# Hybrid encoder layer on one core: the first request's adaLN and projections by channel quarters

## The chip, the cores and the metric

The kernel runs on one core of a Trainium2 chip. The core has five engines that run their own instruction streams: TensorE (PE) for matmuls, VectorE (DVE), ScalarE (ACT), GpSimd (POOL), and SyncE (SP), which issues the DMAs here. The metric is the device time of one launch in microseconds (us), as the median of several runs. Lower is better.

## The reference

Two requests (1024 tokens of 1024 channels each, fp32) go through the same layer. What matters:

```python
mod = silu(c) @ w_ada + b_ada
shift, scale, gate = split(mod, 3)                       # 1024 channels each
h = rms_norm(x, norm_g) * (1 + scale) + shift
qa, ka, va, za, qb, kb, vb, zb, ga, gb = split(h @ w_in) # 512 128 128 512 512 512 512 512 1024 1024
oa = gqa_attention(rope(rms_norm(qa)), rope(rms_norm(ka)), va) * silu(za)   # branch A, 8 heads of 64
lam = exp(sum(lam_q1 * lam_k1)) - exp(sum(lam_q2 * lam_k2)) + lam_init
ob = rms_norm(diff_attention(rope(qb), rope(kb), vb, lam)) * silu(zb)       # branch B, 4 heads
merged = sigmoid(ga) * (oa @ w_proj_a) + sigmoid(gb) * (ob @ w_proj_b)
y = x + gate * (merged @ w_out)
```

`x` comes in transposed as well, so that `h` is made as 8 chunks of 128 channels (partitions) by tokens.

## The kernel before, in words

**Precision.** Most matmuls are made of three fp32r products: an operand is split into a high part (ACT copies it to fp32r) and a low part (DVE or POOL subtracts), and high x high, high x low, low x high are summed. So 8 channel chunks make 24 matmuls for one projection tile. AdaLN and the statistics are plain fp32.

**Stages.** The program does request 0 ("group 0"), then request 1. For a group: the head (`head`: keys and values `kva_gen`, the first half of the branch-A queries `qa_gen`, and some gate projections), attention in six phases (32 units of branch A, in two phases; 16 of branch B, in four), then merge and output. `kva_gen`, `qa_gen` and the branch-B projections work by token tiles (128 tokens by 256 columns, 24 matmuls each, in `proj_tt`, L514); behind the matmuls of a tile come the RMS statistics, rotary positions and transposes on ACT, DVE, POOL and PE. The gate projections (`z_gen`, L703) come in groups of 24 matmuls of 512 columns; 48 groups for a request, whose results go to memory (`zd`) until the merge.

**What sets the order.** `weave` draws matmul streams step by step, each at a share and with a lead from the tables at the top (`Z_SHARE`, `ATT_W`, `IN_A`, `Z_A` ...). It fills PE with projections while attention waits for its softmax. Three steps of `z_gen` are one group. A scheduler then sets the final order on each engine; each engine runs its own list strictly in order.

**The head of group 0.** `start` issues all loads on the SP queue. The shift and scale columns of `w_ada` are loaded as eight tiles of 512 rows by 512 columns (`load_ada`, L250): for channels 0 to 511 the shift, then the scale, then both for channels 512 to 1023. Loads of x (two halves of 512 tokens, `load_xT0`, L242) and the weights of keys and values stand among them. `ada` sums with the 2 columns of `silu(c)` as the stationary operand (L300: 32 matmuls with 2 output rows and 512 columns, each profiled as two instructions); `ada_end` copies the two rows, transposes them with four small matmuls (L309) and adds the bias. `inv_rms` sums the squares of a token half by one-column matmuls with `ones_c` (L273), `spread` broadcasts the result (L287, L289). `modulated` then makes `h` for four chunks at a time (L323 to L329), for the first token half only; `start_late` makes the second half after the first steps of the head. Thus nothing is projected before half of adaLN is done.

**Banks.** PSUM has two score banks of 1024 columns (`sbank`), three others (`fbank`) and one for values. `gbank` draws from both kinds while `alone` is set (outside attention).

## Time and profile before

| | |
|---|---|
| three runs | 1974.46, 1974.42, 1972.81 us; median 1974.42 |
| profiled execution | span 1971.9 us, 30870 instructions; the page gives no other time for it |
| PE | 1901.8 us busy (96%) |
| DVE | 1353.0 us (69%) |
| ACT | 1012.0 us (51%) |
| POOL | 680.9 us (35%) |
| DMA | 295.26 MB, mean 150 GB/s |
| mean granted PE clock | 0.990 |

"Busy" counts from an instruction's start to its modelled end, and matmuls are pipelined, so a PE that is busy all the time may still do little: the start-to-start time of dense matmuls tells their price. PEld is the load of the stationary operand. A row of the group views reads: line, engine, operation, output<-input by the program's names, shapes, count | busy us, mean ns of one | idle time of the engine before them and what ended it. A row of the waits reads: who waited <- for whom: us in total, times, longest.

### The profile page before, as it was taken

What the parts mean: (1) busy time and instruction counts of PE and PEld (TensorE: products, weight loads), DVE (VectorE), ACT (ScalarE), POOL (GpSimd) and SP (SyncE); (2) the same over time, 40 slices, a digit from 0 to 9 for tenths busy, and PEclk for the clock granted to TensorE, in tenths of its full rate; (3) what the DMA queues carried; (4) which work ended last, traced back from release to release, by engine and by line L of the source; (5) the groups of instructions that cost most, each with busy time, mean ns of one, the idle gap of its engine ahead of it and who ended that gap; (6) DMA issues with size and microseconds to landing.
All of it is one profiled execution on the core that took longest, in us unless ns stands there. A gap on an engine that the chain in (4) does not pass through costs nothing. (4 is left out here: it accounts for less than half of the span.)

```text
span 1971.9 us, 30870 instructions
## 1 busy us (share of the span) xinstructions
PE 1901.8 (96%) x10466; PEld 1619.1 (82%) x10466; DVE 1353.0 (69%) x2165; ACT 1012.0 (51%) x1920; POOL 680.9 (35%) x958
## 2 busy tenths in 40 slices
PE   8999999999989999999999999999999999998999
PEld 3888888888878985778889788888888889776887
DVE  4658876786888577757465598768878766776641
ACT  4447655565655353464323576556666444447410
POOL 2363511442446251322235344114444426322210
PEclk9899999999999999999999999999999999999999
DMA  9125545556454345865641355555555334478431
GB/s 315 33 89 149 144 139 149 158 156 174 127 144 111 89 117 173 272 234 179 222 151 44 115 144 167 148 149 157 156 152 161 98 102 119 120 222 267 166 102 75
DMA packets 271614, 295.26 MB, mean 150 GB/s; under 512 B 37856, under 2 KB 220256, under 8 KB 271456
## 3 DMA queue, kind: packets, MB, share of 16 engines
q1 hardware_dynamic: 271456, 293.28, 50.1%
q8 instruction: 84, 1.38, 0.3%
q14 instruction: 74, 0.61, 0.1%
HBM read 133.72 MB, written 42.01 MB: 89 GB/s over the span
## 5 line engine op out<-in xcount | busy, mean ns | idle before, releaser
L703 PE MATMUL f<-u,w 128*128 128x512 f32 x2184 | 561.3, 395 | 3.0 <-ACT w L179 1.3
L514 PE MATMUL f<-w,u 128*128 128x256 f32 x3456 | 489.6, 286 | 5.2 <-ACT ev L709 2.7
L514 PEld LDWEIGHTS f<-w,u 128*128 128x128 f32 x3456 | 460.7, 192 | 26.8 <-ACT ev L709 3.7
L703 PEld LDWEIGHTS f<-u,w 128*128 128x128 f32 x2184 | 396.8, 189 | 78.1 <-ACT w L179 1.8
L181 POOL TENSOR_TENSOR w<-st,w 128x512 fp32r<-128x512 f32 x166 | 227.8, 1391 | 463.2 <-ACT w L179 412.9
L736 DVE TENSOR_REDUCE m<-s 128x1 f32<-128x1024 f32 x256 | 310.2, 1217 | 55.1 <-PE s L735 52.0
L771 DVE STREAM_TRANSPOSE p<-p 128x1024 f32<-128x1024 f32 x192 | 238.0, 1241 | 112.8 <-ACT p L738 110.2
L785 DVE TENSOR_TENSOR q<-q,hi 128x512 fp32r<-128x512 f32 x256 | 193.9, 774 | 47.9 <-ACT hi L784 46.4
L738 ACT ACTIVATE p<-s,m,rsB 128x1024 f32<-128x1024 f32 x128 | 154.0, 1204 | 135.0 <-DVE m L737 103.3
L738 ACT ACTIVATE p<-s,m,rsA 128x1024 f32<-128x1024 f32 x128 | 153.8, 1202 | 128.1 <-DMA q<-p 95.8
L735 PE MATMUL s<-u,sw 128*128 128x512 f32 x512 | 205.0, 401 | 0.0
L784 ACT ACTIVATE hi<-q 128x512 fp32r<-128x512 f32 x256 | 153.2, 624 | 78.2 <-DMA q<-p 50.2
L179 ACT ACTIVATE w<-st 128x512 fp32r<-128x512 f32 x196 | 114.2, 626 | 101.9 <-DMA st<-in_w_in_dram 46.6
L976 PE MATMUL f<-u,w 128*128 128x512 f32 x552 | 136.4, 400 | 11.3 <-ACT ev L709 4.1
L796 PE MATMUL a<-hi,u 128*128 128x256 f32 x512 | 132.0, 284 | 4.8 <-DVE oo L813 3.1
L976 PEld LDWEIGHTS f<-u,w 128*128 128x128 f32 x552 | 104.8, 192 | 35.3 <-DVE u L987 4.6
L836 PE MATMUL a<-q,u 128*128 128x256 f32 x512 | 125.9, 385 | 5.6 <-DMA q<-p 1.9
L797 PE MATMUL a<-q,u 128*128 128x256 f32 x512 | 129.8, 287 | 0.5 <-DVE q L785 0.4
L734 PE MATMUL s<-u 128*128 128x512 f32 x256 | 109.5, 428 | 7.9 <-ACT p L738 4.0
L734 PE MATMUL s<-u,u 128*128 128x512 f32 x256 | 103.3, 404 | 13.8 <-ACT p L738 9.0
L836 PEld LDWEIGHTS a<-q,u 128*128 128x128 f32 x512 | 95.9, 193 | 21.6 <-issue 2.9
L735 PEld LDWEIGHTS s<-u,sw 128*128 128x128 f32 x512 | 97.4, 190 | 15.5
(186 smaller groups left out, 2639.1 us busy)
## 6 DMA issues: line engine op xcount, KB each, us to landing
q<-p SPq DMA_DIRECT2D x768, 128.0 KB, 2.6
st<-in_w_in_dram SPq DMA_DIRECT2D x132, 256.0 KB, 3.0
zd<-ev SPq DMA_DIRECT2D x96, 256.0 KB, 2.2
sw<-u SPq DMA_DIRECT2D x256, 64.0 KB, 2.0
p<-zd SPq DMA_DIRECT2D x64, 256.0 KB, 3.8
u<-in_w_ada_dram SPq DMA_DIRECT2D x8, 1024.0 KB, 10.4
st<-in_w_in_dram SPq DMA_DIRECT2D x64, 128.0 KB, 2.7
st<-in_w_out_dram SPq DMA_DIRECT2D x32, 256.0 KB, 3.2
```

Source lines behind the costliest of these rows:

```text
L181: e.tensor_tensor(out=wl, in0=st, in1=wh.bitcast(F32), op=ALU.subtract)
L514: nc.tensor.matmul(ps, lt[c][:, sl], w[:, c, wi, :], start=(k == 0), stop=(k == 23))
L703: nc.tensor.matmul(ps, w[:, c, wi, e * P : (e + 1) * P], rt[c], start=(k == 0), stop=(k == 23),)
L734: nc.tensor.matmul(s[:, sl], q, k[:, sl], start=True, stop=False)
L735: nc.tensor.matmul(s[:, sl], sw, k[:, sl], start=False, stop=True)
L736: nc.vector.tensor_reduce(out=m, in_=s, axis=AX.X, op=ALU.max, negate=True)
L738: nc.scalar.activation(pt.rearrange("p (j c a) -> p j c a", j=4, c=8), s.rearrange("p (c a j) -> p j c a", c=8, j=4), AF.Exp, scale=rs, bi ...
L771: nc.vector.transpose(pt, pt)
L784: nc.scalar.activation(th, tl.bitcast(F32), AF.Copy)
L785: nc.vector.tensor_tensor(out=tl, in0=tl.bitcast(F32), in1=th.bitcast(F32), op=ALU.subtract)
L836: nc.tensor.matmul(acc, u["v"][:, k], pT[:, k], start=(k == 0), stop=(k == 7))
L976: nc.tensor.matmul(ps, w[:, c, wi, d * P : (d + 1) * P], o[:, oi, :], start=(k == 0), stop=(k == 11))
```

## The change

AdaLN is done by quarters of 256 channels. `load_ada` loads, for a quarter, 512 rows by 256 columns of the shift and 256 of the scale into one tile. `ada` then gives each of four 128-row chunks its own 32-column strip of the PE array (`tile_position`), with `silu(c)` padded to 32 columns (`cpad`, in the `at` tile); the four partial sums land on four partition strips, are copied as one 128 x 512 tile, and are added and transposed by matmuls with `two`, a matrix of ones at rows j*32 and j*32+1. As soon as a quarter of shift and scale is there, `modulated` makes two chunks of `h` (the multiplication by 1/rms is inside it now, on DVE or POOL), and those two chunks are at once multiplied: `chunk_early` sums keys and values of all eight token tiles in the two score banks, `z_early` two gate groups (first 256 columns, first token half) in two of the other banks. Both token halves go this way (the second from quarter 1 on), so `start_late` is gone. `kva_gen` and the first `z_gen` take these sums as `given`; the weights of the second gate piece are loaded into two `u` tiles. While early sums are held, `gbank` draws only from `fbank`. The squares of the second half are added before the one-column products, as those of the first half were. The tables of shares and leads are set anew for both groups.

```diff
 Z_SHARE = (
-    (7, 19, 5, 3, 3, 4),
+    (6, 19, 5, 3, 2, 6),
     (9, 14, 7, 3, 2, 6),
 )
-    (1.15, 1.354, 1.035, 1.15, 0.85, 1.069),
+    (1.15, 1.188, 1.035, 1.15, 0.991, 1.069),
...
+Z_FIRST = (12, 6)
+Z_FIRST_A = (-0.15, 0.0)
...
-BEHIND = 1.4
-AHEAD = 100
+BEHIND = 1.45
+AHEAD = 99
...
-        if alone[0] and turn[0] % 5 in (0, 2):
+        if alone[0] and not early and turn[0] % 5 in (0, 2):
...
+    def ada(quarter, wts, cpad):
+
+        acc = gbank()
+        for q, wt in enumerate(wts):
+            for c in range(4):
+                nc.tensor.matmul(
+                    acc[32 * c : 32 * c + 32], cpad[:, q * 4 + c], wt[:, c], start=(q == 0), stop=(q == 1),
+                    tile_position=(0, 32 * c),
+                )
+        part = rtile()
+        nc.vector.tensor_copy(part, acc)
+        ps = gbank()[:, :8].rearrange("p (t c g) -> p t c g", t=2, g=2)
+        for third in range(2):
+            for c in range(2):
+                o = third * 256 + c * P
+                nc.tensor.matmul(ps[:, third, c], part[:, o : o + P], two, start=True, stop=True)
...
+    def chunk_early(ht, hf, c):
+
+        hh, hl = (x[c] for x in ht[hf][:2])
+        w = kva_w[0][0]
+        for tt in (1, 0, 3, 2) if c == NCH - 1 else range(4):
+            sl = slice(tt * P, (tt + 1) * P)
+            for k, (lt, wi) in enumerate(((hh, 0), (hh, 1), (hl, 0))):
+                first, last = c == 0 and k == 0, c == NCH - 1 and k == 2
+                mm = nc.tensor.matmul(
+                    early["kva"][hf * 4 + tt], lt[:, sl], w[c][:, wi, :],
+                    start=(first and tt % 2 == 0), stop=(last and tt % 2 == 0),
+                )
...
+        wts = [load_ada(n) for n in range(2)]
         kva_w.append(load_w(w_cols(w_in, (C_KA, 256)), early=True))
-        wts += [load_ada(n) for n in range(5, 8)]
+        wts += [load_ada(n) for n in range(2, 4)]
+        kva_w.append(load_w(w_cols(w_in, (C_ZA, 256)), early=True))
         xT.append(load_xT0(1))
...
+        wts += [load_ada(n) for n in range(4, 6)]
+
+        rsb = [spread(inv_rms(added(squares(xT[0]))))]
+        kva = [x[:, i : i + 256] for x in (sbank(), sbank()) for i in range(0, 1024, 256)]
+        early.update(kva=kva, z=[fbank(), fbank()])
+        for quarter in range(4):
+            ada(quarter, wts[quarter * 2 : quarter * 2 + 2], cpad)
+            if quarter < 2:
+                split_early(kva_w[quarter][1])
+            for hf in range(2):
+                if quarter == 0 and hf:
+                    continue
+                if quarter in ((0, 2), (1, 2))[hf]:
+                    add_h(ht, hf, quarter // 2)
+                    if hf and quarter == 1:
+                        rsb.append(spread(inv_rms(added(squares(xT[1])))))
+                cs = range(0 if hf and quarter == 1 else quarter * 2, quarter * 2 + 2)
+                modulated(ht, hf, xT[hf], cs, rsb[hf])
+                for c in cs:
+                    chunk_early(ht, hf, c)
+            for c in (range(0), range(4), range(4, 6), range(6, 8))[quarter]:
+                z_early(ht, c)
+            if quarter == 0:
+                wts += [load_ada(n) for n in range(6, 8)]
...
-            for i in range(2):
-                weave((islice(kva, 6), 6, 0.0), (islice(zs, 3), 3, 0.0))
-                if i == 0:
-                    late()
-            weave((chain(kva, qa), 40, 0.0), (islice(zs, nz - 6), nz - 6, Z_HEAD_A[g]))
+            drain(islice(zs, 6))
+            weave((kva, 27, 0.0), (islice(zs, Z_FIRST[0]), Z_FIRST[0], Z_FIRST_A[0]))
+            weave((qa, 27, 0.0), (islice(zs, Z_FIRST[1]), Z_FIRST[1], Z_FIRST_A[1]))
```

The order on the engines. First the SP queue at the end of the loads of the head, before: all adaLN tiles and x stand ahead of the tables (`gqa` to `p_1427`, the vectors of lambda).

```order
L250 DMA u_192<-in_w_ada_dram 128x4x512
L242 DMA u_194<-in_xT_prompt_dram 128x2x512 x2
L242 DMA u_195<-in_xT_prompt_dram 128x2x512 x2
L407 DMA gqa<-in_qn_a_dram 128x64
L407 DMA gka<-in_kn_a_dram 128x64
L441 DMA tab_396<-in_cosA_dram 128x8x64
L441 DMA tab_398<-in_sinA_dram 128x8x64
```

The same queue in the change, from the rotary tables of branch B on; `u_309` and `u_312` are the last adaLN quarter.

```order
L452 DMA cosB<-in_cosB_dram 128x8x16 x2
L452 DMA sinB<-in_sinB_dram 128x8x16 x2
L454 DMA gB<-in_qn_b_dram 128x64
L454 DMA gB<-in_kn_b_dram 128x64
L464 DMA p_1469<-in_lam_q_dram 128x64
L464 DMA p_1469<-in_lam_k_dram 128x64
L464 DMA p_1469<-in_lam_q_dram 128x64
L264 DMA u_309<-in_w_ada_dram 128x4x256 x2
L264 DMA u_312<-in_w_ada_dram 128x4x256 x2
L464 DMA p_1469<-in_lam_k_dram 128x64
L473 DMA subg<-in_subln_g_dram 128x1
```

The last adaLN quarter has moved behind all tables but the fourth lambda vector and `subg`.

DVE in the head, before: the last shift and scale (`modc`), the modulation of the last chunks (`u_170`) and their low parts (`u_332`) stand ahead of the branch-B tables and lambda.

```order
L313 TENSOR_TENSOR modc<-s_324,bcol 128x8
L317 TENSOR_TENSOR modc<-modc,gcol 128x8
L325 TENSOR_SCALAR u_170<-u_170,modc 128x512 x2
L329 TENSOR_TENSOR u_332<-u_170,u_331 128x512 x4
L181 TENSOR_TENSOR w_412<-st_417,w_412 128x2x256
L416 TENSOR_SCALAR gB<-gB 128x64
```

DVE in the change, from the copy of quarter 2's sums (`f_494`; quarters count from 0) to that of quarter 3's (`f_592`).

```order
L318 COPY row_503<-f_494 128x512
L466 TENSOR_TENSOR p_1469<-p_1469 128x128
L474 TENSOR_SCALAR subg<-subg 128x1
L469 TENSOR_REDUCE lam_116<-p_1469 128x2
L471 TENSOR_TENSOR nlam<-lam_116 128x1
L472 TENSOR_SCALAR nlam<-nlam 128x1
L326 TENSOR_TENSOR modc<-f_505,bcol 128x2x4
L329 TENSOR_TENSOR modc<-modc,gcol 128x4
L341 TENSOR_SCALAR u_171<-u_171,modc 128x512
L341 TENSOR_SCALAR u_203<-u_203,modc 128x512
L318 COPY row_601<-f_592 128x512
```

The lambda steps now stand between quarter 2's sums and the modulation of its chunks (`u_171` of the first token half, `u_203` of the second).

More of the change, by code (lines that the diff above doesn't have):

```diff
@@ L118 @@
     alone = [True]
+    early = {}
     turn = [0]
@@ L207, in load_w @@
                 split_w(w, q, st)
-        return (w, sts) if early else w
+        cols = [w[c // 2][:, c % 2] for c in range(NCH)]
+        return (cols, (w, sts)) if early else cols
     def w_cols(mat, *cols):
@@ L337, in add_h, with z_early @@
             part.extend(u[:, c] for c in range(4))
+    def chunk_early(ht, hf, c):
[8 more added lines that the diff above has]
+                    start=(first and tt % 2 == 0), stop=(last and tt % 2 == 0),
+                )
+                if first and tt % 2 or last and tt % 2 == 0:
+                    tc.keep_in_program_order(mm)
+    def z_early(ht, c):
+        hh, hl = (x[c] for x in ht[0][:2])
+        w = kva_w[1][0]
+        for e in range(2):
+            for k, (wi, rt) in enumerate(((0, hh), (0, hl), (1, hh))):
+                nc.tensor.matmul(
+                    early["z"][e], w[c][:, wi, e * P : (e + 1) * P], rt,
+                    start=(c == 0 and k == 0), stop=(c == NCH - 1 and k == 2),
+                )
     def start(ht):
+        cpad = mtile("at", [P, 256], bufs=1).rearrange("p (c m) -> p c m", c=NCH)
+        nc.vector.memset(cpad, 0.0)
         nc.scalar.activation(cT, ccol, AF.Silu)
-        wts = [load_ada(n) for n in range(2)]
+        nc.vector.tensor_copy(cpad[:, :, :2], cT)
         dma(bcol, t["b_col"])
@@ L502, in ht_gen, with proj_tt @@
             yield 1
-    def proj_tt(ht, w, tt):
+    def proj_tt(ht, w, tt, given={}):
+        if tt in given:
+            for _ in CUTS:
+                yield 1
+            if tt == NTT - 1:
+                early.pop("kva")
+            return given[tt]
         ps = fbank()[:, :256]
@@ L1090, in z_item @@
         if i < 2:
-            return z_gen(ht, C_ZA + i * 256, st["zd"], i * 2, fn)
+            col, w = C_ZA + i * 256, None
+            if early and i == 1:
+                w = load_w(w_cols(w_in, (col, 256)), room=(utile(), utile()))
+            return z_gen(ht, col, st["zd"], i * 2, fn, w)
         if i < 4:
@@ L1099 @@
     states = [new_state(0), new_state(1)]
[L1100 removed]
+    start(states[0]["ht"])
     load_tables()
```

146 lines of the change are left out of this document (59 added, 87 removed).

## The prediction

> **What bounds the kernel now.** I first read the busy time by stretches. The cuts are the first dense sums (42.4), the clock's recovery (60), the first scores (140.7), the fifth attention unit (176.3) and the last of the 32 branch-A units (514.8); columns are length, busy us of PE, PEld, DVE, ACT, POOL (instructions), granted clock, DMA share, GB/s.
>
> ```profile
> 0.00:42.40 42.40, 34.82 (x102) 9.23 (x102) 18.20 (x31) 17.18 (x29) 7.84 (x12) 1.00 1.01 357
> 42.40:60.00 17.60, 17.60 (x92) 16.72 (x91) 9.08 (x24) 7.28 (x12) 4.94 (x4) 0.62 0.34 81
> 60.00:140.70 80.70, 73.84 (x497) 67.89 (x495) 48.73 (x135) 40.11 (x105) 45.27 (x63) 0.98 0.16 50
> 140.70:176.30 35.60, 35.60 (x195) 31.05 (x196) 25.89 (x38) 24.54 (x39) 8.54 (x12) 0.95 0.51 139
> 176.30:514.80 338.50, 331.08 (x1939) 290.29 (x1938) 255.15 (x371) 203.00 (x392) 113.48 (x144) 1.00 0.55 153
> 514.80:593.80 79.00, 72.84 (x423) 63.76 (x422) 65.24 (x106) 44.57 (x90) 38.72 (x69) 0.96 0.49 131
> ```
>
> From 60 us on PE is busy nearly all the time and no other engine comes close: 331 of 338.5 us in the long stretch, where DVE has 255. Before 42.4 us the DMA engines are full. A busy PE there says little, so I next read what it runs, in the timeline of PE (start, length, line, count):
>
> ```profile
> 30.15 10.46 PE L300 MATMUL f<-u,cT 128*2 128x512 f32 x24
> 42.41 2.31 PE L514 MATMUL f<-w,u 128*128 128x256 f32 x12
> 47.23 8.09 PE L273 MATMUL f<-ones_c,q 128*128 128x1 f32 x50
> 55.18 4.19 PE L703 MATMUL s<-u,w 128*128 128x512 f32 x9
> 59.17 2.08 PE L514 MATMUL f<-w,u 128*128 128x256 f32 x12
> 97.34 5.18 PE L703 MATMUL f<-u,w 128*128 128x512 f32 x22
> 102.36 2.79 PE L514 MATMUL f<-w,u 128*128 128x256 f32 x22
> 111.57 3.14 PE L514 MATMUL f<-w,u 128*128 128x256 f32 x24
> 114.55 0.62 PE L703 MATMUL f<-u,w 128*128 128x512 f32 x2
> ```
>
> Up to 42.4 us PE runs only adaLN (L300) and statistics, no projection. Then 50 one-column sums (L273) take 8 us. From start to start, a dense gate matmul (L703) takes (102.36-97.34)/22 = 0.23 us and a dense projection matmul (L514) (114.55-111.57)/24 = 0.124 us. The same lines by stretch (first L514, then L703):
>
> ```profile
> 0.00:60.00 60.00, 5.73 (x27) 5.47 (x28) 0.89 0.81 276
> 60.00:140.70 80.70, 48.01 (x359) 46.28 (x357) 0.98 0.16 50
> 0.00:60.00 60.00, 4.19 (x9) 2.86 (x9) 0.89 0.81 276
> 60.00:140.70 80.70, 28.15 (x111) 19.88 (x111) 0.98 0.16 50
> ```
>
> So by 60 us PE has done 27 x 0.124 + 9 x 0.23 = 5.4 us of the work that has to be done anyway. From 60 to 140.7 it does 359 x 0.124 + 111 x 0.23 = 70.0 us of it in 80.7. The hole in this kernel is the first 60 us; behind it PE is the bound, so whatever matmuls are moved into the hole should come off the end.
>
> **What the change puts into the hole.** Keys and values (8 token tiles x 24 = 192 matmuls) and two gate groups (48) are summed as the quarters come: 192 x 0.124 + 48 x 0.23 = 34.8 us of PE work. AdaLN keeps its 64 profiled instructions, 16 a quarter. When is the last quarter done? That decides. First the transfers: the SP queue's timeline, one stretch of DMA, and the issues with their time to landing.
>
> ```profile
> 22.66 5.40 SPq L242 DMA_DIRECT2D u<-in_xT_prompt_dram x4
> 39.03 1.09 SPq L413 DMA_DIRECT2D cosB<-in_cosB_dram x2
> 45.53 0.35 SPq L425 DMA_DIRECT2D p<-in_lam_q_dram x1
> 46.87 0.43 SPq L425 DMA_DIRECT2D p<-in_lam_k_dram x1
> 30.00:35.00 5.00, 5.00 (x16) 1.15 (x16) 4.71 (x6) 1.70 (x3) 3.46 (x2) 1.00 1.05 409
> p<-in_lam_k_dram SPq DMA_DIRECT2D x2, 32.0 KB, 3.2
> ```
>
> At 409 GB/s 1 MB takes 2.56 us. Today all 14 MB stand ahead of the tables. DMAs take turns on eight semaphores, so an issue waits for the eighth before it, and the first cosB issue waits until 39.03 for the last piece of x. In the change only 12 MB stand ahead: 5.1 us less, and I add 1.1 us because the three small column loads now go ahead of the first big one. So cosB issues at about 35, and the first lambda vector 6.5 us later, as today, less 0.5 for the load of `subg` that moves behind: 41. Three lambda loads take 1.3, and then the last adaLN quarter is issued, at 42.3. Its 2 MB need 5.1 us and some 2 us to start (between nothing and the 3.2 us of a small load): landed at 49.4. The fourth lambda vector is issued behind it and lands right after, about 50. Nothing is gained by the shorter head of the queue: the last adaLN quarter arrives 10 us later than the last byte of today's 14 MB.
>
> **Who waits for that.** In DVE's new order the product of the lambda vectors, their reduction, and the subtraction that waits for ACT's exponential stand ahead of the shift and scale of quarter 2 (third of four), and those ahead of the copy of quarter 3's sums. Today's rows for this chain:
>
> ```profile
> 51.40 0.28 DVE L427 TENSOR_TENSOR p<-p 128x128 f32<-128x128 f32 x1
> 55.44 0.28 DVE L430 TENSOR_REDUCE lam<-p 128x2 f32<-128x128 f32 x1
> 55.75 0.20 ACT L431 ACTIVATE lam<-lam 128x2 f32<-128x2 f32 x1 [1.98 <-DVE lam L430]
> 56.41 0.15 DVE L433 TENSOR_SCALAR nlam<-nlam 128x1 f32<-128x1 f32 x1
> L329 DVE TENSOR_TENSOR u<-u,u 128x512 fp32r<-128x512 f32 x8 | 5.0, 680 | 1.1 <-ACT u L328 1.1
> L328 ACT ACTIVATE u<-u 128x512 fp32r<-128x512 f32 x8 | 4.5, 616 | 0.4 <-DVE u L325 0.4
> L325 DVE TENSOR_SCALAR u<-u,modc 128x512 f32<-128x512 f32 x4 | 2.0, 539 | 0.0
> L306 DVE COPY p<-f 2x512 f32<-2x512 f32 x3 | 2.0, 676 | 1.4 <-PE f L300 1.0 <-issue 0.4
> ```
>
> Reduction to end is 56.56-55.44 = 1.1 us, plus 0.3 for the product: lambda 50 to 51.4. Quarter 2 then takes 0.3 for its shift and scale (two L313/L317-sized steps), two modulations of 0.54, and 0.62 on ACT until its first matmuls can start, at about 53. (The first two quarters' 17.4 us of sums have some 30 us ahead of that.) DVE goes on with the copy of quarter 3 (0.68), four low parts (2.7), shift, scale and one weight split (1.1), two modulations (1.1), four low parts (2.7): 61. PE has two quarters left, each 48 x 0.124 + 12 x 0.23 = 8.7 us: 53 + 17.4 = 70, which DVE's 61 doesn't hold up. What is left of the head (6 gate groups, 144 x 0.23 = 33.1; 8 query tiles, 192 x 0.124 = 23.8; transposes about 2.5) is 59.4 us. Today's named waits of PE between 60 us and the first scores are these:
>
> ```profile
> PE f L514 <- ACT ev L709: 2.3, 1, 2.3
> PE s L734 <- DVE u L570: 2.1, 1, 2.1
> PE f L567 <- DVE row L556: 1.7, 2, 1.5
> PE f L567 <- POOL row L556: 0.7, 1, 0.7
> ```
>
> That is 6.8 us. I keep 5: the one before the first scores stays, and keys now come all at once to be normalised, with 6 gate groups on PE to cover them. First scores: 70 + 59.4 + 5 = 134.5, against 140.7: **6 us**. If that cover fails, POOL's share (45 us busy in this stretch now) comes into the path; 7 us more is the bound I allow. If no wait is left it is 5 us less.
>
> **What is done by then.** All 8 gate groups (192) stand ahead of the first scores, against 120 matmuls today: 72 x 0.23 = **16.6 us** that the attention phases no longer have to carry. They give it back only where PE is their bound. The first four units fall from 66 gate matmuls to 24 (and gain 6 projection ones): 8 us less for PE in a stretch of 35.6 in which DVE has 26 us, in a chain; I take half, so 4 are lost. The stretch at 514.8 to 593.8 gains 24 gate matmuls where PE has 6 us of idle time: 4 come back. New weights and leads move matmuls between other stretches with the same total. PE's idle time from 176.3 to 593.8 is 13.6 us, which bounds what they can win; I take 0, with 6 either way.
>
> **Other edits.** The square sums are added on DVE before one matmul for each tile, so 28 of the 32 one-column products of the second half go (part of L273's 8 us, inside the hole). The padded adaLN weights, the row `two`, the `mc` steps and the separate row tile cost under 2 us of DVE, beside transfers. The room for the second gate piece's weights in two `u` tiles moves its loads to rows that wait for nothing on PE. Nought for each; if the cover is gone, up to 2.
>
> AdaLN's column tiles have no row of before. Run one after another they cost 24 instructions in 10.46, so 0.43 x 16 = 6.9 us a quarter; side by side at best a quarter of that, 1.7. For the last quarter the second half counts, 3.4 or 0.9 us behind 49.4: 52.8 at worst against DVE's 51.4 for lambda, under 2 us on the path. I take 0. The Trainium skill (TensorE: Matmul & The Clock Gate, Part 3) measured 2.38 times for three column tiles of 32; by that, as an estimate, a quarter takes 2.9 us and the sum is unchanged. It also (TensorEngine Tiling (Array Packing), Key Properties) says that a change of tiling mode drains the array, which speaks against alternating such tiles with full matmuls; it gives no price, and no run here shows it yet.
>
> The clock: from 55.18 nine L703 took 59.17-55.18 = 4.0 us, 0.44 each, at the 0.62 mean of that stretch. Quarter 2's sums start after a wait, so some 3 us of them may run at half rate, 1.5 us. I count it in the 5 us of waits. The Trainium skill (TensorE: Matmul & The Clock Gate, Part 1) says an idle window of about 3.4 us halves the clock and a busy one restores it; by that it costs, as an estimate, 1.7 us for each restart, and only the last restart is on the path.
>
> **Sum.** 6 + 16.6 - 4 + 4 = 22.6 us off the span of 1971.9: 1949.3. The page has no time for the profiled execution beside its span; the median of the runs, 1974.42, is 2.5 above it. Forecast **1952**, own range 1944 to 1959.
>
> **The rivals.** *The tables don't hold the last quarter* (0.2): quarter 2 is modulated before lambda, and PE starts at about 45 on what has landed; the early sums then end at 62, 8 us earlier: 1944. For it: nothing in the data needs lambda. Against it: DVE runs in order, and the product is ahead.
>
> *The head stays as long* (0.13): with both score banks and two of three other banks held by early sums, one bank serves transposes, spreads and the next gate group; the waits of 6.8 us double, and the last quarter slips by the 7 us allowed. First scores at 143; only the 16.6 come, less 4: 1971.9 + 2 - 12.6 + 2.5 = 1964.
>
> *The attention phases are full twice over* (0.08), and this one is slower: where PE work falls, DVE's chain keeps the old time; where it rises, PE lengthens it. From the order, in stretches of four units, the stretches that gain matmuls sum to 10.5 us in the first group and 12.6 in the second (one has 25 gate matmuls more). 1971.9 - 6 + 23.1 + 2.5 = 1991. It decides from where the shortened stretches return under 17 of their losses. Against it: DVE's 255 of 338.5 us.
>
> *The change does nothing in the hole* (0.04): the early sums wait for one buffer until all of h is there; 1971 to 1975.
>
> **How the numbers follow.** The forecast holds 0.55. 0.2% is 3.9 us, about what a measurement tells from no change: faster means under 1970.5. Forecast, first and second rival are on that side: 0.88; same 0.04; slower 0.08. The range takes in the first two rivals with their half widths, 1938 to 1967.
>
> **What would show it.** Right: projection matmuls on PE from about 20 us, a DVE wait for the lambda load near 50, early sums ended near 70, first scores at 130 to 139, the 32 branch-A units of the first group 10 to 18 us shorter. Wrong: first scores after 141, or a second group that is more than 5 us longer.

## The result, and the profile after

The changed kernel takes 1972.49 us (median of 12 runs, 1970.91 to 1980.13); the kernel before took 1974.54 beside it. The ratio on record is 0.9998 (the two medians alone would give 0.9990), with a 95% interval of 0.9988 to 1.0009: no difference. The forecast was 1952, so the prediction was wrong. The profiled execution has a span of 1971.0 us, against 1971.9 before.

First the busy time by stretches of the changed kernel (columns as in the prediction: length, busy us of PE, PEld, DVE, ACT, POOL, granted clock, DMA share, GB/s). The cuts are where PE becomes dense (46.6), the first sums of quarter 2 (67), the first scores (145.6), the fifth unit, the 33rd, and group 0's tail from 746.5 up to group 1's first scores (1093.2); the stretch from the 33rd unit to the 36th stands ahead of that from the 33rd to the 44th, which holds it.

```profile
0.00:46.60 46.60, 22.08 (x116) 14.86 (x117) 27.30 (x35) 19.16 (x33) 18.55 (x20) 0.85 0.98 304
46.60:67.00 20.40, 19.51 (x117) 13.81 (x117) 14.32 (x29) 8.15 (x13) 6.89 (x4) 0.92 0.42 119
67.00:145.60 78.60, 76.40 (x482) 68.50 (x483) 47.96 (x125) 35.14 (x94) 41.32 (x59) 1.00 0.23 71
145.60:182.30 36.70, 29.15 (x166) 25.18 (x165) 29.58 (x44) 22.77 (x45) 16.75 (x21) 0.92 0.47 118
182.30:509.40 327.10, 322.62 (x1900) 283.73 (x1899) 258.51 (x372) 197.82 (x382) 106.75 (x138) 1.00 0.60 155
509.40:589.20 79.80, 74.91 (x438) 65.88 (x437) 63.22 (x103) 44.43 (x89) 37.98 (x66) 0.98 0.51 131
509.40:746.50 237.10, 230.52 (x1392) 204.10 (x1390) 176.66 (x296) 121.94 (x249) 110.77 (x205) 0.99 0.44 114
746.50:1093.20 346.70, 333.74 (x1653) 273.48 (x1653) 213.41 (x366) 149.10 (x270) 106.58 (x119) 0.99 0.57 182
1093.20:1971.00 877.80, 844.87 (x4610) 728.95 (x4608) 607.10 (x907) 451.26 (x829) 286.38 (x404) 0.99 0.53 146
```

The last two stretches of the kernel before, for comparison:

```profile
747.80:1096.00 348.20, 338.02 (x1671) 274.67 (x1670) 216.76 (x372) 148.38 (x274) 107.05 (x119) 1.00 0.55 182
1096.00:1971.90 875.90, 843.99 (x4610) 726.21 (x4608) 606.28 (x907) 451.68 (x829) 282.43 (x404) 0.99 0.50 146
```

The first scores come at 145.6, 4.9 us later than before, not 6 earlier. From there to the end it is 1825.4 us against 1831.2: 5.8 shorter, where 16.6 was forecast. So half of the 21.7 us that are missing lie in the head (10.9), half behind it (10.8). Behind the head PE is busy 1878.9 - 22.1 - 19.5 - 76.4 = 1760.9 us, against 1775.5 before, so 14.6 us of work did go; but it idles 64.5 us in place of 55.7, and that takes 8.8 back.

**The head.** PE's timeline in the changed kernel (start, length, line, count; in brackets the idle time before and what ended it). L363 are the early key and value sums, L376 the early gate sums, L313 and L323 adaLN, L289 and L303 the second half's statistics.

```profile
39.94 4.23 PE L363 MATMUL s<-w,u 128*128 128x256 f32 x22 [0.84 <-DVE u L345]
44.02 0.95 PE L289 MATMUL f<-ones_c,q 128*128 128x1 f32 x8
46.60 1.11 PE L303 MATMUL f<-ident,rs 128*128 128x128 f32 x4 [1.63 <-POOL rs L296]
47.37 6.90 PE L376 MATMUL f<-u,w 128*128 128x512 f32 x24
54.20 1.92 PE L313 MATMUL f<-u,at 128*32 128x512 f32 x14
57.88 5.76 PE L363 MATMUL s<-w,u 128*128 128x256 f32 x46
63.48 0.95 PE L323 MATMUL f<-two,row 128*128 128x2 f32 x8
66.96 0.50 PE L363 MATMUL s<-w,u 128*128 128x256 f32 x2 [0.34 <-ACT u L344]
82.23 2.91 PE L376 MATMUL f<-u,w 128*128 128x512 f32 x12
```

The early key and value sums (L363) up to 46.6 us are these; of the early gate sums (L376) none has run by then:

```profile
0.00:46.60 46.60, 9.92 (x48) 8.72 (x48) 0.85 0.98 304
```

So at 46.6 us 48 of the 240 early matmuls are done: the first token half's two quarters, and nothing else. From then on PE is full (19.5 of 20.4 us, then 76.4 of 78.6). The second half's sums of the first two quarters come at 56 to 63.6, and quarter 2's adaLN product (L323) stands behind them in PE's order. So quarter 2 starts at 67, not at 53, and the early sums end at 85, not at 70. From there the rest of the head takes 60.5 us, where 59.4 of work and 5 of waits were forecast: that step was right to 4 us, on the good side.

**What holds the second half.** ACT's and DVE's timelines on its statistics and modulation:

```profile
30.41 2.17 ACT L273 ACTIVATE q<-u 128x512 f32<-128x512 f32 x4
36.18 0.81 ACT L339 ACTIVATE u<-u,modc 128x512 f32<-128x512 f32 x1 [3.60 <-DVE modc L329]
...
38.98 1.14 ACT L273 ACTIVATE q<-u 128x512 f32<-128x512 f32 x2
```

```profile
48.38 5.79 DVE L337 TENSOR_TENSOR u<-u,row 128x512 f32<-128x512 f32 x4 [3.21 <-ACT row L305]
60.46 0.29 DVE L469 TENSOR_REDUCE lam<-p 128x2 f32<-128x128 f32 x1
```

After four of eight squares ACT stands 3.6 us before a modulation of the first half, and the other four squares come behind it and end at 40.1; DVE adds them up to 42.4; the column sums then stand behind 22 projection matmuls on PE (44.02), the power on POOL, the spread and its copy follow, and only at 48.4 does DVE begin the second half's four multiplications. The lambda vectors, on which the forecast let quarter 2 hang, are reduced at 60.5 and done before 61.4, two microseconds ahead of the product that quarter 2 waits for.

**The attention phases.** The gate matmuls by stretch (their count in brackets): L752 in the changed kernel in the first four units and the next 28, then L703 in the kernel before in the same two:

```profile
145.60:182.30 36.70, 6.13 (x24) 4.24 (x24) 0.92 0.47 118
182.30:509.40 327.10, 162.18 (x624) 111.54 (x624) 1.00 0.60 155
```

```profile
140.70:176.30 35.60, 17.73 (x66) 12.85 (x66) 0.95 0.51 139
176.30:514.80 338.50, 169.20 (x654) 117.59 (x654) 1.00 0.55 153
```

The first four units have 42 gate matmuls fewer (42 x 0.23 = 9.7 us) and take 1.1 us more: PE idles 7.6 us there, where it idled none, at a granted clock of 0.92. Of this, 4.2 us are one wait of the scores (L785) for the low parts of transposed tiles on DVE (L615), and 2.0 one for ACT's exponential (L789). The next 28 units take 11.4 us less for 30 fewer (6.9 us). From unit 33 to 44 it is 4.1 more, in the tail 1.5 less, in group 1 it is 1.9 more: 1.1 - 11.4 + 4.1 - 1.5 + 1.9 = -5.8, as above.

### The profile page after: what moved, and what is told of

It reads as the page before. It is cut to its first block, busy times and chain, and to the rows that moved or that the text cites. A ratio compares the mean times of both kernels' runs of the same rounds, so it can differ in the third digit from the quotient of the medians.

```text
span 1971.0 us, 30811 instructions
## 1 busy us (share of the span) xinstructions
PE 1878.9 (95%) x10426; PEld 1612.6 (82%) x10426; DVE 1374.8 (70%) x2170; ACT 1005.3 (51%) x1913; POOL 694.0 (35%) x966
## 4 chain that ended last, share of the span: by engine, by line
PE 57%; DVE 13%; DMA 10%; SPq 7%; issue 5%; ACT 4%; POOL 3%; ACTq 0%; DVEq 0%; POOLq 0%
PE f L559 12%; PE f L752 12%; DMA q<-p 6%; PE f L1056 6%; SPq L827 5%; PE f L1027 5%; PE a L887 4%; PE s L785 4%; PE s L786 3%; PE s L1056 3%; DVE m L787 3%; DVE q L836 3%; DVE p L822 2%; PE s L1027 2%; PE a L847 1%
## 5 line engine op out<-in xcount | busy, mean ns | idle before, releaser
L752 PE MATMUL f<-u,w 128*128 128x512 f32 x2136 | 551.2, 395 | 2.7 <-ACT w L186 1.7
L559 PE MATMUL f<-w,u 128*128 128x256 f32 x3264 | 458.3, 285 | 1.5 <-DVE ssB L911 0.8
L559 PEld LDWEIGHTS f<-w,u 128*128 128x128 f32 x3264 | 432.4, 191 | 21.0 <-DVE ssB L911 1.0
L752 PEld LDWEIGHTS f<-u,w 128*128 128x128 f32 x2136 | 386.2, 188 | 75.8 <-ACT w L186 2.9
L188 POOL TENSOR_TENSOR w<-st,w 128x512 fp32r<-128x512 f32 x162 | 220.6, 1382 | 394.6 <-ACT w L186 312.1
L787 DVE TENSOR_REDUCE m<-s 128x1 f32<-128x1024 f32 x256 | 310.7, 1217 | 50.1 <-PE s L786 46.6
L789 ACT ACTIVATE p<-s,m,rsB 128x1024 f32<-128x1024 f32 x128 | 154.0, 1204 | 146.2 <-DVE m L788 99.0
L789 ACT ACTIVATE p<-s,m,rsA 128x1024 f32<-128x1024 f32 x128 | 153.8, 1202 | 127.6 <-DMA q<-p 88.3
L186 ACT ACTIVATE w<-st 128x512 fp32r<-128x512 f32 x188 | 109.2, 625 | 80.5 <-DMA st<-in_w_in_dram 30.7
L887 PE MATMUL a<-q,u 128*128 128x256 f32 x512 | 129.6, 391 | 11.7 <-DVE oo L864 4.3
L1027 PE MATMUL f<-u,w 128*128 128x512 f32 x540 | 132.1, 397 | 3.8 <-ACT ev L758 3.8
L848 PE MATMUL a<-q,u 128*128 128x256 f32 x512 | 130.1, 287 | 4.1 <-DVE q L836 4.1
L1027 PEld LDWEIGHTS f<-u,w 128*128 128x128 f32 x540 | 102.4, 191 | 25.5 <-ACT ev L758 4.2
L785 PE MATMUL s<-u,u 128*128 128x512 f32 x256 | 104.0, 407 | 14.2 <-ACT p L789 8.5
L614 ACT ACTIVATE u<-f 64x256 fp32r<-64x256 f32 (+1 forms) x202 | 73.0, 362 | 80.9 <-DVE u L615 64.1
L785 PE MATMUL s<-u 128*128 128x512 f32 x256 | 109.6, 428 | 2.4 <-ACT p L789 2.3
```

The lines of the kernel that those rows point to most:

```text
L188: e.tensor_tensor(out=wl, in0=st, in1=wh.bitcast(F32), op=ALU.subtract)
L559: nc.tensor.matmul(ps, lt[c][:, sl], w[c][:, wi, :], start=(k == 0), stop=(k == 23))
L752: nc.tensor.matmul(ps, w[c][:, wi, e * P : (e + 1) * P], rt[c], start=(k == 0), stop=(k == 23),)
L785: nc.tensor.matmul(s[:, sl], q, k[:, sl], start=True, stop=False)
L787: nc.vector.tensor_reduce(out=m, in_=s, axis=AX.X, op=ALU.max, negate=True)
L789: nc.scalar.activation(pt.rearrange("p (j c a) -> p j c a", j=4, c=8), s.rearrange("p (c a j) -> p j c a", c=8, j=4), AF.Exp, scale=rs, bi ...
```

## The experiments

Theory 1: the head is late because the second token half's statistics and modulations are late, so that the early sums cannot use the time before 46.6. Its rival is the prediction's own step: the last adaLN quarters, behind tables and lambda vectors, hold it. Theory 2: behind the head the time lies in how gate and projection matmuls are spread, which the tables set; its rival is that the tables matter little.

**ada_first.** The last adaLN quarter is loaded with the third, ahead of all tables.

```diff
-        wts += [load_ada(n) for n in range(4, 6)]
+        wts += [load_ada(n) for n in range(4, 8)]
```

> The changed kernel with the loads of the last adaLN quarter issued with those of the third, so ahead of all tables and of the lambda vectors on SP. Theory 'late loads' (the step of the prediction: tables and lambda hold the last quarters): the last quarter lands near 52 in place of 58.5, the early sums end at 76 to 79 in place of 85, first scores at 137 to 140, time 1964 to 1967. Theory 'second half's statistics' (the sums of quarters 2 and 3 stand behind the second half's first sums, which wait for its statistics): early sums still end at 84 to 86, time 1970 to 1974.

Measured: 1971.17 us, ratio 0.9991 (0.9981 to 1.0002). SP's and PE's timelines:

```profile
26.02 12.44 SPq L264 DMA_DIRECT2D u<-in_w_ada_dram  x8
```

```profile
64.05 0.95 PE L323 MATMUL f<-two,row 128*128 128x2 f32 x8
82.81 2.91 PE L376 MATMUL f<-u,w 128*128 128x512 f32 x12
```

All eight loads are issued by 38.5, ten microseconds sooner than the last in the changed kernel (48.95), and quarter 2's product comes at 64.05 in place of 63.48, the end of the early sums at 85.7. So the late loads don't hold the head of the changed kernel, and the total is the rival's, too (1970 to 1974).

**stat_once.** The second half's statistics left out.

```diff
-                        rsb.append(spread(inv_rms(added(squares(xT[1])))))
+                        rsb.append(rsb[0])
```

> The changed kernel without the statistics of the second token half: its squares, their additions, the reciprocal root and its spread are left out, and the row of the first half is used. Theory 'second half's statistics': the second half's first sums start near 50 in place of 56.3, the early sums end at 77 to 80, first scores at 138 to 141; time 1964 to 1967 if the head's gain passes to the end, 1969 to 1973 if the attention phases absorb it. Theory 'late loads': quarter 2 still starts at 66 or 67, the early sums end at 84 to 86, no change of time beyond 2 us.

Measured: 2023.79 us, ratio 1.0253 (1.0232 to 1.0274). PE's timeline in the head:

```profile
41.38 3.28 PE L363 MATMUL s<-w,u 128*128 128x256 f32 x26
55.59 1.05 PE L323 MATMUL f<-two,row 128*128 128x2 f32 x8 [0.81 <-DVE row L318]
59.17 0.79 PE L363 MATMUL s<-w,u 128*128 128x256 f32 x2 [0.56 <-ACT u L344]
71.89 1.05 PE L323 MATMUL f<-two,row 128*128 128x2 f32 x8 [0.82 <-DVE row L318]
79.04 0.39 PE L363 MATMUL s<-w,u 128*128 128x256 f32 x2
```

The first half of the theory is shown: without its statistics the second half's sums start at 41.4 in place of 56.3, all sums of the first two quarters are done at 52.9 in place of 63.6, and quarter 2's product and sums come at 55.6 and 59.2 in place of 63.5 and 67.0. Among PE's waits from 50 to 90 us the profile names no load. But the end of the early sums doesn't follow: they end at 87.7, where 77 to 80 was expected. Half of quarter 3's adaLN matmuls stand behind quarter 2's sums in PE's order and run only at 70.0; copy, product and modulation follow, and quarter 3's sums start at 79.0, with 18 matmuls of a later gate group ahead of them. So the statistics are not the only hold: with them gone, in this order, the last quarter's own chain takes their place.

For the total the run says little. The edit set off another order in the whole first group: 216 gate and 453 projection matmuls lie ahead of its first scores, at 169.7, where the changed kernel has 192 and 384.

**x1_first.** The second half of x loaded ahead of the gate piece's weights.

```diff
-        kva_w.append(load_w(w_cols(w_in, (C_ZA, 256)), early=True))
         xT.append(load_xT0(1))
+        kva_w.append(load_w(w_cols(w_in, (C_ZA, 256)), early=True))
```

> The changed kernel with the second token half of x issued ahead of the gate piece's weights on SP, instead of behind them. Theory 'second half late' (until 46.6 us PE has done only 48 of the 240 early sums, because the second half of h is not there; from then on it is full): the second half's squares, 30.4 now, start 3 to 4 us sooner, its first sums at 51 to 53 in place of 56.3, the early sums end at 80 to 82 in place of 85, first scores at 141 to 143. Theory 'PE order and ACT hold it, not the data': early sums still end at 84 to 86. Total: 1967 to 1972 by the first, 1970 to 1975 by the second (a change of a few units' order costs up to 5 either way).

Measured: 2001.58 us, ratio 1.014 (1.0124 to 1.0155). In the head the early sums end 1.9 us sooner (next rows), at 83.3, between the two expectations, and the first scores come at 143.8. ACT's squares end at 32.7 in place of 40.1, but DVE's additions of them stand behind quarter 1's copy and end at 39.5. The column sums then start at 39.63 in place of 44.02, but the spread, behind 24 projection matmuls on PE, only at 45.79 in place of 46.60. The data came sooner, and the orders of DVE and PE kept most of it.

```profile
39.63 1.84 PE L289 MATMUL f<-ones_c,q 128*128 128x1 f32 x8 [3.31 <-DVE q L281]
80.35 2.91 PE L376 MATMUL f<-u,w 128*128 128x512 f32 x12
```

Yet the total is 29 us longer. Its stretches from the fifth to the 33rd unit and from there to the 45th:

```profile
181.10:532.00 350.90, 338.58 (x1963) 296.02 (x1963) 262.50 (x380) 201.56 (x392) 110.88 (x157) 0.99 0.56 146
532.00:773.30 241.30, 226.30 (x1329) 197.83 (x1327) 172.77 (x287) 118.33 (x240) 101.08 (x186) 0.97 0.42 109
```

Units 5 to 32 take 23.8 us more for 24 gate and 38 projection matmuls more (5.5 + 4.7 = 10.2 us); units 33 to 44 take 4 us more for 24 and 38 fewer. PE idles 12.3 and 15.0 us there against 4.5 and 6.6. In units 5 to 32 PE's longest wait in sum is now that of a unit's scores (L785) for ACT's exponential (L789). First the row of the changed kernel, then of this run (us in total, times, longest):

```profile
PE s L785 <- ACT p L789: 1.4, 2, 1.3
PE s L785 <- ACT p L789: 7.6, 6, 2.1
```

Two loads were exchanged, and the attention phases, whose order the scheduler then set anew, lost more than the whole forecast gain.

**fused_first.** `modulated` as one DVE operation and a shift on ACT, no multiplications on POOL, on top of ada_first.

```diff
-            e.tensor_tensor(out=xT[c], in0=xT[c], in1=rsb, op=ALU.mult)
...
+            nc.vector.scalar_tensor_tensor(out=xT[c], in0=xT[c], scalar=scale, in1=rsb, op0=ALU.mult, op1=ALU.mult)
+            nc.scalar.activation(xT[c], xT[c], AF.Identity, bias=shift)
```

> The changed kernel with each modulation as one DVE operation with two multiplications and an addition of the shift on ACT (no multiplications on POOL), and with the last adaLN loads ahead of the tables. Theory 'DVE and POOL hold the second half': the four low parts that take 1.45 to 1.71 us beside POOL now fall to 1.0 to 1.1 and the second half's first sums start at 51 to 54 in place of 56.3; early sums end at 79 to 83; first scores 140 to 143. Rival, that the statistics (POOL's power at 45.5, spread to 47.75) hold it: early sums end at 84 to 86. Total 1966 to 1972 by the first, 1970 to 1975 by the rival.

Measured: 1985.25 us, ratio 1.0056 (1.0041 to 1.0072). DVE's and PE's timelines:

```profile
47.52 2.73 DVE L336 SCALAR_TENSOR_TENSOR u<-u,modc,row 128x512 f32<-128x512 f32 x4
```

```profile
80.81 2.91 PE L370 MATMUL f<-u,w 128*128 128x512 f32 x12
```

Four of these operations take 2.73 us, where four multiplications alone (the expectation calls them low parts) took 5.79. The second half's sums start at 53.3 in place of 56.3, as expected; the early sums end at 83.7 and the first scores come at 143.5, 0.5 to 0.7 us later than expected. The total was missed, by the attention phases again. So theory 1 holds in part. The statistics hold the second half and quarter 2, but at the end of the early sums no edit gave the 15 us: 2.0 from the one-step modulation (83.7 against ada_first's 85.7), 1.9 from the earlier x, and some 1.5 from leaving the statistics out, if the 18 later gate matmuls (4.1 us) that stand ahead of that end are taken off.

**tabs_old** (the changed kernel with the old tables) and **tabs_new** (the kernel before with the new ones). The core of the edit, and its reverse for tabs_new:

```diff
-    (6, 19, 5, 3, 2, 6),
+    (7, 19, 5, 3, 3, 4),
...
-    (0.996, 1.046, 1.1, 1.105, 0.945, 1.52),
+    (1.07, 0.837, 1.1, 0.95, 1.07, 1.52),
```

> The changed kernel with the seven tables of before (shares, weights, leads, BEHIND 1.4, AHEAD 100); its head stays as changed. If the retuned tables matter little (my retune term of 0, 6 either way): 1969 to 1976 us. If the new tables give the head's gain back, because they leave the first four units only 24 gate matmuls: 1963 to 1968. If on the contrary only the new tables keep the changed kernel level: 1977 to 1985.

> The kernel before with the tables of the change (its head has no column quarters and 6 gate groups, and stays so). If the new tables are only made for the new head, in which two more gate groups are done: slower than before by 5 to 20 us, 1979 to 1994. If they are better by themselves: 1960 to 1972, and the new head is then what loses. If they don't matter: 1970 to 1978.

Measured: 1994.52 us, ratio 1.0107 (1.0085 to 1.0129), and 1993.65 us, ratio 1.0095 (1.0076 to 1.0114). Each set of tables costs some 20 us with the other head: tabs_new came as expected of tables made for the new head (1979 to 1994), tabs_old beyond all three ranges. For tabs_old the tail of group 0:

```profile
764.50:1115.00 350.50, 332.12 (x1627) 267.55 (x1626) 216.37 (x375) 155.32 (x276) 103.09 (x116) 0.99 0.56 177
```

With two gate groups done early and the phases still drawing 37 groups, the tail has 191 gate matmuls, 43 (9.9 us) short of the changed kernel's 234, and still takes 350.5 us in place of 346.7: PE idles 18.4 us there in place of 13.0. Units 33 to 44 idle 13.0 in place of 6.6. Gate matmuls are what PE does while attention and the tail wait; done early, they leave holes where they were. For tabs_new it is the other way round: its phases draw two groups fewer while its head still does only six, so 282 gate matmuls are left for a tail that had 236 before, and that takes 365.0 us in place of 348.2.

**old_share**: tabs_old, with the new shares alone.

> The changed kernel with the old weights, leads, BEHIND and AHEAD, but with the new gate shares (35 groups in the first five phases in place of 37). With all old tables it took 1994.5, and 191 gate matmuls were left behind unit 43 where before and the change have 236 and 234. Theory 'the two gate groups done in the head are missing at the end': the tail has 234 again, loses 8 to 12 us of idle time, and u32 to u43 as much: 1972 to 1982. Theory 'weights and leads': still 1988 to 1996.

Measured: 1989.5 us, ratio 1.0085 (1.0067 to 1.0103). The tail has its 234 gate matmuls again and idles 348.90 - 337.08 = 11.8 us in place of 18.4, but the 28 units take 341.6 us in place of 327.1 for 6 gate and 8 projection matmuls more (2.4 us):

```profile
180.60:522.20 341.60, 328.96 (x1916) 287.16 (x1915) 256.87 (x371) 198.60 (x387) 107.87 (x138) 1.00 0.57 148
```

The shares account for 5 of the 22 us; the rest is in the weights, the leads and the two scheduler offsets (`BEHIND`, `AHEAD`), which no run separates. The expectation that put it on the missing groups fell.

**fill** (more gate groups in the first phase, from the second) and **gates6** (6 gate groups in the head, 8 in the first phase).

```diff
-    (6, 19, 5, 3, 2, 6),
+    (9, 16, 5, 3, 2, 6),
...
-    (0.0, 0.05, 0.2, 0.0, 0.0, 0.1),
+    (0.2, 0.05, 0.2, 0.0, 0.0, 0.1),
```

> The changed kernel with 9 and 16 gate groups in the first two attention phases in place of 6 and 19, and with a lead of 0.2 for those of the first phase in place of 0. Theory 'the first four units lack fill' (they take 36.7 us for 25.6 us of PE work): they carry 60 to 72 gate matmuls in 36 to 39 us, the 33rd unit's first scores come 6 to 9 us earlier than 509.4, time 1963 to 1967. Theory 'the phases are set by DVE's chain, whatever PE has': the 33rd unit within 2 us of 509.4, time 1970 to 1975.

```diff
-    (6, 19, 5, 3, 2, 6),
+    (8, 19, 5, 3, 2, 6),
...
-Z_FIRST = (12, 6)
+Z_FIRST = (6, 6)
```

> The changed kernel with 6 gate groups woven into its first head in place of 8, the two others in the first attention phase (8 in place of 6, lead 0.2). Theory 'gate sums are fill that the first four units need' (these have 7.6 us of idle PE, and a clock of 0.92): the idle time there falls under 3 us and the total to 1963 to 1969. Theory 'work done in the head is worth its 11 us wherever it is taken from': no gain, 1971 to 1976.

Measured: 1980.73 us, ratio 1.0042 (1.0026 to 1.0057), and 2006.03 us, ratio 1.0168 (1.0142 to 1.0193). For fill the first four units, then units 5 to 32; for gates6 the same two:

```profile
145.90:184.00 38.10, 33.83 (x174) 28.64 (x173) 28.48 (x42) 22.22 (x41) 11.78 (x15) 0.91 0.54 139
184.00:520.00 336.00, 328.10 (x1926) 287.12 (x1925) 261.75 (x377) 200.36 (x390) 111.06 (x150) 0.99 0.58 149
```

```profile
155.90:192.10 36.20, 35.78 (x215) 31.50 (x214) 27.70 (x45) 23.52 (x42) 11.72 (x19) 1.00 0.49 124
192.10:539.80 347.70, 336.21 (x1943) 293.04 (x1942) 261.59 (x373) 200.29 (x391) 112.80 (x152) 0.99 0.56 145
```

What was expected of the first four units came: with 65 gate matmuls (fill) they take 38.1 us, with 58 (gates6) 36.2 and 0.4 us of idle time, with 24 (the change) 36.7. So these units have a length of their own, and gate matmuls are free in them up to about 60. But the gain did not reach the end. Units 5 to 32 of fill have 32 gate matmuls fewer than the changed kernel's and 54 projection ones more, 0.7 us less in sum, and take 8.9 us more. In gates6 24 projection matmuls moved ahead of the first scores, which come at 155.9, and the 28 units take 20.6 us more for 624 and 624 (38 more, 4.7 us). The totals hoped for (1963 to 1967 and 1963 to 1969) were missed, and those of the rivals (1970 to 1976) as well: a table that mends one stretch moves the order of all that follow.

**z_fx.** To test whether a shorter head pays when the order behind it stays: ada_first, x1_first and fused_first together, and the early gate sums of a quarter ahead of the second half's work. Behind the head PE's order then stays near the changed kernel's, with the same tables.

```diff
                 for c in cs:
                     chunk_early(ht, hf, c)
-            for c in (range(0), range(4), range(4, 6), range(6, 8))[quarter]:
-                z_early(ht, c)
+                if hf == 0:
+                    for c in (range(0), range(4), range(4, 6), range(6, 8))[quarter]:
+                        z_early(ht, c)
```

> The changed kernel with a shorter head: second half of x ahead of the gate piece's weights, last adaLN loads ahead of the tables, one-step modulation on DVE, and the early gate sums of a quarter ahead of the second half's work. Behind the head PE's order stays within a few matmuls of the changed kernel's (u32 to u35 hold the same 81 gate and 172 projection matmuls). Theory 'the head's microseconds pass to the end if the order behind it is kept': early sums end at 78 to 81 in place of 85, first scores at 139 to 142, time 1965 to 1969. Theory 'whatever is won ahead is lost behind it': 1971 to 1976.

Measured: 1968.27 us (12 runs), ratio 0.9981 (0.9969 to 0.9994): faster than before by 0.1 to 0.3%, and the lowest median of all, though ada_first's interval (0.9981 to 1.0002) overlaps with it. PE's timeline, and the first two stretches behind its first scores:

```profile
32.73 3.04 PE L370 MATMUL f<-u,w 128*128 128x512 f32 x12
72.00 4.38 PE L745 MATMUL f<-u,w 128*128 128x512 f32 x18 [0.26 <-DVE modc L326]
```

```profile
143.30:174.00 30.70, 26.45 (x149) 22.95 (x148) 25.58 (x38) 19.82 (x38) 12.62 (x16) 0.89 0.47 118
174.00:504.80 330.80, 324.40 (x1917) 285.43 (x1916) 260.19 (x379) 200.09 (x389) 109.18 (x143) 1.00 0.60 155
```

Early gate sums now run at 33 us, before the second half's statistics. The early sums end at 84.9, no sooner, but 18 matmuls of the next gate group (4.4 us) are done among them. The first scores come at 143.3, the fifth unit at 174.0 (182.3 in the changed kernel), the 33rd at 504.8 (509.4), the end 3.4 us sooner. The expected 139 to 142 for the first scores was missed, the expected total was met. With the order nearly kept, 8.3 us won by the fifth unit left 4.6 at the 33rd and 3.4 at the end; with the order changed, x1_first and fused_first won 2 in the head and lost 31 and 13 behind it. These are single executions, and runs of one kernel lie up to 10 us apart, so the 3.4 alone would prove little.

How far an order differs can be counted in the traces: the gate and the projection matmuls on PE between the first scores of one branch-A unit and those of the next, for the 32 units of group 0, against the changed kernel. Four runs have its 648 gate matmuls in these units, and its 658 projection ones to within 13. In ada_first every unit has the same counts as there, and in z_fx the differences sum to 146, none of them behind unit 18: the 32 units take 361.7 and 361.5 us, against 363.8. In z_x1_fit (next) and stat_once the differences sum to 281 and 683: they take 376.3 and 384.4. So nearly the same work in another order costs 12 and 21 us.

**z_x1_fit.** Can the order be fitted by hand? x1_first with the early gate sums moved as in z_fx, and two weights set so that the counts of matmuls in each stretch come near the changed kernel's.

```diff
-    (0.996, 1.046, 1.1, 1.105, 0.945, 1.52),
+    (1.05, 1.09, 1.1, 1.105, 0.945, 1.52),
```

> The kernel that lost most in its attention phases, the one with x's second half first (2000), with the early gate sums ahead of the second half's work and with two weights of the first group's phases set so (1.05 and 1.09 for 0.996 and 1.046) that the gate and projection matmuls of each stretch come near the changed kernel's again (85 and 161 in units 32 to 35, where x1_first had 59 and 137). Theory 'the tables' fit is worth some 20 us and any change of the head unsets it': 1964 to 1975. Theory 'x first costs by itself': above 1990.

Measured: 1995.15 us, ratio 1.0116 (1.0099 to 1.0133). Its head is longer (first scores at 149.5), and the 28 units take 340.3 us for 624 gate and 591 projection matmuls, where the changed kernel takes 327.1 for 624 and 586:

```profile
185.50:525.80 340.30, 331.27 (x1916) 289.25 (x1917) 257.80 (x374) 199.21 (x387) 108.05 (x141) 0.99 0.57 149
```

Equal counts in a stretch are not enough. The number is that of the rival "x first costs by itself" (above 1990), but z_fx loads x first as well and takes 1968, so the load alone is not the cause. PE's wait of the scores for ACT's exponential is 6.3 us in these 28 units, against 1.4. The place of each matmul between the units differs, as counted above, and with it the order on the other engines; which places do the harm was not settled.

## Why the prediction was wrong, point by point

**That PE is the bound behind 60 us: right, but read too far.** "Whatever matmuls are moved into the hole should come off the end": 72 gate matmuls did come off behind the head, and PE's busy time there fell by 14.6 of 16.6 us. PE idles 8.8 us more instead. PE was 97% busy behind the head with that work in that order; a busy PE there did not mean that less work would take less time, because part of what is taken away becomes waiting.

**The last adaLN quarter at 49.4 and lambda at 50: late, and not the bound.** At 349 GB/s instead of 409 (below) everything on the queue came later: the first cosB issue at 40.8 instead of 35, that of the last adaLN quarter at 49.0 instead of 42.3. (The reading that the cosB issue waited for x was not exact: in the kernel before, the last piece of x had landed at 37.8, and the issue at 39.03 followed straight on three weight loads, issued from 34.91 to 38.99.) But ada_first took that away and the head did not get shorter. The rival "the tables don't hold the last quarter" (1944) was right that they don't, and wrong that PE would then start quarter 2 at about 45: in stat_once lambda comes behind quarter 2's modulation, and the early sums still end at 87.7.

**"The first two quarters' 17.4 us of sums have some 30 us ahead of that": the step that failed in the head.** Only 48 matmuls (6 us) had been done at 46.6, and the second half's were late by its own chain of statistics on four engines, which the prediction did not cost at all: it priced only what was taken out of the statistics. stat_once shows this cause: without the chain, these 17.4 us are done at 52.9, as the prediction had it. It also shows that an early quarter 2 alone does not give 70: 53 + 17.4 takes for granted that the last two quarters' sums run on without a break. In the changed kernel they do, because quarter 3's adaLN matmuls run at 64.69, ahead of quarter 2's sums; in stat_once's order half of them stand behind these. Quarter 2 came 14 us late and the early sums 15. The rest of the head then took 60.5 us, not 64.4: first scores at 145.6, 11.1 after the forecast. By the numbers this is the rival "the head stays as long", whose 143 was nearest, with another cause than the banks it named. The rival "the change does nothing in the hole" (1971 to 1975) has the measured total, but by luck: early sums did run as quarters came, and 72 gate matmuls went ahead of the first scores.

**The first four units, 4 us lost: mis-sized.** 9.7 us of gate matmuls went and the stretch became 1.1 longer. gates6 has 58 gate matmuls there in 36.2 us, so that many fit for nothing, and the whole of the work taken away was lost, not half.

**24 more gate matmuls in units 33 to 36 for little: right.** The stretch takes 79.8 us against 79.0 for 5.5 us more work, though units 37 to 44, with 22 fewer, take 3.3 us more; the forecast had nothing for them.

**"New weights and leads move matmuls between other stretches with the same total ... I take 0, with 6 either way": the term mis-sized most.** The bound of 6 came from PE's idle time before, which limits what a new table can win. It says nothing of what a wrong one costs: with the new head and the old tables the kernel takes 1994.5, so the new tables are worth 22 us, and without them the change would have been 20 us slower than before. The tables fit one head each, and no sum of a head's worth and a table's worth gives the result. The slower rival (1991, phases that are full twice over) comes near tabs_old by its number, and in part by its mechanism: PE idles where work fell. With the tables of the change it did not rule.

**The signs.** First scores after 141 were named as a sign of being wrong, and came. A sign of being right came too: the 32 branch-A units of the first group are 10.3 us shorter (363.8 against 374.1, forecast 10 to 18). But they hold 72 gate matmuls, 16.6 us, less.

## What to carry to other kernels

Before counting work moved into an idle stretch as gained, follow the slowest of the inputs it needs, here the second token half's statistics through ACT, DVE, PE and POOL, and ask how much of it can run before PE is full anyway. Work that fills waits is worth its duration only if the stretch it leaves is bound by the same engine; count the idle time it will leave there. And in a kernel with a tuned order the order is itself a term of the sum, here 7 to 31 us behind the head in the runs that changed it, more than the edits gave: keep it as near as can be when an edit is to be judged, as z_fx did, and count how near it is.

## What the runs showed of the hardware

Four column strips of PE run side by side, as their rate shows: L313's 14 profiled instructions take 1.92 us (0.14 each; 16 take the same 1.92 at 64.69) where before 24 took 10.46 (0.44 each). That is 3.2 to 3.6 times; the Trainium skill (TensorE: Matmul & The Clock Gate, Part 3) has 2.38 for three strips. A quarter takes 1.9 us at full clock, the low end of the forecast's 1.7 to 6.9.

A DVE operation with two tensor inputs is slowed by a like one on POOL: L337's four take 5.79 us (1.45 each) while POOL runs its own four, from 48.42 for 6.89 us; in fused_first, with no multiplication on POOL, a step that does more takes 0.68 each. The Trainium skill (SBUF — State Buffer, SBUF: two separate sides) says that such a DVE operation and a reading one on GpSimd hold a shared port in turn, each for a whole instruction; the doubled time agrees with it.

```profile
48.42 6.89 POOL L337 TENSOR_TENSOR u<-u,row 128x512 f32<-128x512 f32 x4 [1.88 <-ACT row L305]
```

The adaLN loads have rows of 1 KB now (256 columns) where they had 2 KB, and the full DMA engines move 349 GB/s where they moved 409:

```profile
20.00:25.00 5.00, 2.90 (x16) 1.15 (x16) 4.97 (x6) 0.43 (x1) 5.00 (x4) 0.75 1.09 349
```

The other loads of that time differ too, so that the row size alone does it was not tried.
